# The gates' projections by Strassen's scheme on quarters, with two of four weight sums per block made by adding transfers

## The chip, the cores and the metric

One Trainium2 chip, one core of it. The metric is the time of one launch on the device in microseconds (us). The kernel before takes 1664.78 us, the median of 3 runs (1664.39 to 1664.81).

## What is computed

One layer of a decoder trunk over 512 tokens of width 2048, in fp32: a conditioned RMSNorm, one wide projection, two parallel mixers, gates, an output projection and a last RMSNorm.

```python
shift, scale, gate = split(silu(c) @ W_ada + b_ada)
h = rmsnorm(x, attn_norm_g) * (1 + scale) + shift
q_lat, kv_lat, k_rope, z_mla, u, v, z_sgu, g_mla, g_sgu = split(h @ w_in)
# widths:  768, 512, 64, then 2048 each for the last six
q  = rmsnorm(q_lat) @ w_uq            # 16 heads, 128 plain + 64 rotary
kv = rmsnorm(kv_lat) @ w_ukv          # 16 heads, 128 keys + 128 values
y_mla = causal_attention(q, rope(k), v) * silu(z_mla)
mixed = tril(w_spatial) @ rmsnorm(v) + b_spatial   # per chunk of 128 tokens, per group
y_sgu = u * mixed * silu(z_sgu)
merged = sigmoid(g_mla) * y_mla + sigmoid(g_sgu) * y_sgu
out = rmsnorm(x + gate * (merged @ w_out))
```

The change concerns the five "gates", of 2048 columns each: z_mla, g_mla, u, z_sgu and g_sgu. The code calls them types 0 to 4, and the kernel after calls them z, g, u, s, t. Each is h (512 x 2048) times a 2048 x 2048 part of w_in.

## The kernel before

**Number format.** Every fp32 matrix product is made of three matmuls of a reduced format: each operand x is a high part (`hi`, a cast on ACT) and a low part (`lo = x - hi`, a subtraction on DVE), and hi·hi + hi·lo + lo·hi is summed in PSUM. `mm3` (lines 134 to 136) issues the three.

**The stream of weights.** A `Stream` holds a list of weight granules in the order of their use; a granule is 128 x 1024 fp32 (512 KB) in the gates. SP issues its transfer into a raw tile (L76, `wraw`, 3 buffers), ACT casts it to `whi` (L97), DVE subtracts to `wlo` (L98), and PE uses the pair (2 buffers). `get(i, ahead=1)` splits one granule ahead of the one whose matmuls come next, and fills the free raw tiles.

**Stages**, by the time in the profiled execution:

- 0 to 74 us: the first columns of the latents, while DVE makes `shift` and `scale` from W_ada (`ada_dot`, 1 MB granules).
- 74 to 142: the rest of the latents; h is normalised and split on the way (`hh`, `hl`, 16 tiles of 128 x 512).
- 142 to 327: the v columns, in groups of 512, 512, 384, 384 and 320 columns.
- 327 to about 1203: the gates, 15 heads one after the other in this stage. A head has five types, a type two granules, and a granule 8 chunks of 128 x 128 weights, each times a 128 x 512 chunk of h: 16 x 3 matmuls of 512 columns a type, 240 a head. What is not of the gates lies beside: `shift_share` (L125: raw granules of the latents' weights times `shift`), the rotary tables (`rope_part`, small DVE operations, L122, L125, L129, L131), the SGU's mix (`sgu_prep`, `sgu_mix`, L675, L676), and from head 8 on the latents' norms.
- Then head 15's types t = 3, 4 (2 x 48 matmuls), the attention, head by head, and from about 1440 the output projection.

**Order.** The program's order is written by hand: each engine runs its own instructions in the order in which the code issues them. `pend` holds evacuations that run one granule later, `bg` the background steps, one for each granule. `evac` (L697 to 712) takes a type's 128 x 512 result out of PSUM: ACT makes the sigmoid, DVE multiplies it in. The gates' results are channel-major (channels on partitions) and stay in SBUF (`gt`, `vt`). All transfers go out from SP; POOL issues none.

## Time and profile before

| what | us |
|---|---|
| median of 3 runs | 1664.78 |
| the profiled execution | 1664.88 |
| its span | 1663.2 |
| PE busy in the span | 1651.6 |
| DVE busy | 947.5 |
| ACT busy | 583.3 |
| POOL busy | 2.2 |
| gates, 327.5 to 1200: the window, PE busy in it, DVE busy in it | 872.5, 872.5, 409.6 |

The profile is of one execution of the program. The busy time of an engine is the union of its instructions' times; PE's matmuls overlap in a pipeline, so a row's own duration (0.39 us for a matmul of 512 columns) is longer than the distance from one start to the next, and the distance is what a matmul costs. DVE's rows have such a tail too, of some 0.08 us. In the rows, `out<-in` gives the program's names of the tiles. A bracket at the end of a row tells how long the engine had been idle before and who ended that.

### The profile page before, as it was taken

How to read it: one execution, taken by the hardware profiler on the slowest of the kernel's cores; microseconds unless marked ns; L12 is line 12 of the kernel's file. 1: busy time of each engine (PE TensorE's matmuls, PEld its weight loads, DVE VectorE, ACT ScalarE, POOL GpSimd, SP SyncE). 2: the span in 40 equal slices, each digit the busy share in tenths (PEclk: the TensorE clock that was granted, in tenths of full speed). 3: DMA queues.
4: the chain of work that ended last, by engine and by line, in shares of the span. 5: the costliest groups of instructions: out<-in, count | busy, mean ns of one | idle time of the engine just before them, and what ended most of it. 6: DMA issues, size and time to landing. Idle time of an engine off the chain costs nothing.

```text
span 1663.2 us, 20082 instructions
## 1 busy us (share of the span) xinstructions
PE 1651.6 (99%) x8024; PEld 1406.1 (85%) x8024; DVE 947.5 (57%) x1456; ACT 583.3 (35%) x967; POOL 2.2 (0%) x11
## 2 busy tenths in 40 slices
PE   9999999999999999999999999999999999999998
PEld 7888889988888888888888888888898888888887
DVE  8988646365665644444443533323578778874453
ACT  4343333234223322221223322222455555542332
POOL 0000000000000000000000000000000000000000
PEclk9999999999999999999999999999999999999999
DMA  9878557344444333322222222232311221126332
GB/s 379 346 295 303 193 211 269 101 151 143 142 152 132 120 137 127 123 102 89 98 92 102 89 101 100 90 102 81 96 61 58 63 75 55 61 77 253 127 101 101
DMA packets 64508, 228.63 MB, mean 137 GB/s; under 512 B 7304, under 2 KB 9376, under 8 KB 57632
## 3 DMA queue, kind: packets, MB, share of 16 engines
q1 hardware_dynamic: 64416, 227.37, 38.7%
q8 instruction: 62, 1.02, 0.2%
q14 instruction: 30, 0.25, 0.0%
HBM read 223.14 MB, written 4.20 MB: 137 GB/s over the span
## 4 chain that ended last, share of the span: by engine, by line
PE 98%; DMA 1%; DVE 0%; ACT 0%; issue 0%; SPq 0%; DVEq 0%
PE ps L135 32%; PE ps L134 32%; PE ps L136 32%; PE ps L947 1%; PE ps L675 1%; PE ps L910 1%; PE ps L911 1%; DMA wraw<-in_w 1%; PE ps L676 0%; DMA wada<-in_c 0%; PE ps L606 0%; DVE wlo L98 0%; ACT whi L97 0%; PE ps L446 0%; DVE wada L122 0%
## 5 line engine op out<-in xcount | busy, mean ns | idle before, releaser
L98 DVE TENSOR_TENSOR wlo<-wraw,whi 128x1024 fp32r<-128x1024 f32 (+3 forms) x304 | 339.0, 1115 | 577.4 <-ACT whi L97 566.4
L134 PE MATMUL ps<-hh,whi 128*128 128x512 f32 x1640 | 641.6, 391 | 0.2 <-ACT hh L389 0.2
L135 PE MATMUL ps<-hl,whi 128*128 128x512 f32 x1640 | 638.5, 389 | 0.8 <-DVE hl L125 0.8
L136 PE MATMUL ps<-hh,wlo 128*128 128x512 f32 x1640 | 638.4, 389 | 0.0
L97 ACT CAST whi<-wraw 128x1024 fp32r<-128x1024 f32 (+3 forms) x304 | 293.7, 966 | 801.6 <-PE ps L135 561.0
L136 PEld LDWEIGHTS ps<-hh,wlo 128*128 128x128 f32 x1640 | 307.8, 188 | 64.5 <-DVE wlo L98 0.2
L135 PEld LDWEIGHTS ps<-hl,whi 128*128 128x128 f32 x1640 | 308.0, 188 | 64.0 <-DVE hl L125 1.1
L134 PEld LDWEIGHTS ps<-hh,whi 128*128 128x128 f32 x1640 | 307.9, 188 | 63.7 <-ACT hh L389 0.6
L134 PE MATMUL ps<-whi,hh 128*128 128x512 f32 (+3 forms) x448 | 148.9, 332 | 0.0
L135 PE MATMUL ps<-wlo,hh 128*128 128x512 f32 (+3 forms) x448 | 148.6, 332 | 0.1
L136 PE MATMUL ps<-whi,hl 128*128 128x512 f32 (+3 forms) x448 | 148.5, 332 | 0.0
L125 DVE SCALAR_TENSOR_TENSOR wada<-wada,cact 128x2048 f32<-128x2048 f32 x47 | 107.2, 2281 | 1.2 <-DMA wada<-in_wada 1.2
L135 PEld LDWEIGHTS ps<-wlo,hh 128*128 128x128 f32 x448 | 84.6, 189 | 5.4 <-DVE wlo L98 0.4
L136 PEld LDWEIGHTS ps<-whi,hl 128*128 128x128 f32 x448 | 84.6, 189 | 5.0
L134 PEld LDWEIGHTS ps<-whi,hh 128*128 128x128 f32 x448 | 84.6, 189 | 5.0
L134 PE MATMUL ps<-whi,b 128*128 128x512 f32 (+1 forms) x212 | 81.8, 386 | 0.0
L135 PE MATMUL ps<-wlo,b 128*128 128x512 f32 (+1 forms) x212 | 81.6, 385 | 0.0
L136 PE MATMUL ps<-whi,g 128*128 128x512 f32 (+1 forms) x212 | 81.6, 385 | 0.0
L134 PEld LDWEIGHTS ps<-whi,b 128*128 128x128 f32 x212 | 39.8, 188 | 7.9
L135 PEld LDWEIGHTS ps<-wlo,b 128*128 128x128 f32 x212 | 39.8, 188 | 7.9
L136 PEld LDWEIGHTS ps<-whi,g 128*128 128x128 f32 x212 | 39.8, 188 | 7.9
L139 ACT CAST lat<-ps 128x512 fp32r<-128x512 f32 (+1 forms) x64 | 35.4, 570 | 13.4 <-PE ps L136 13.3
(229 smaller groups left out, 1340.8 us busy)
## 6 DMA issues: line engine op xcount, KB each, us to landing
wraw<-in_wh SPq DMA_DIRECT2D x150, 512.0 KB, 3.3
wada<-in_wada SPq DMA_DIRECT2D x47, 1024.0 KB, 5.9
wraw<-in_w SPq DMA_DIRECT2D x32, 512.0 KB, 3.5
wraw<-in_wo SPq DMA_DIRECT2D x32, 512.0 KB, 3.3
wraw<-in_w SPq DMA_DIRECT2D x32, 320.0 KB, 2.9
wraw<-in_wv SPq DMA_DIRECT2D x16, 512.0 KB, 3.2
wraw<-in_wv SPq DMA_DIRECT2D x16, 384.0 KB, 3.3
wraw<-in_wq SPq DMA_DIRECT2D x16, 384.0 KB, 2.9
```

Source lines behind the costliest of these rows:

```text
L97: self.nc.scalar.copy(hi[:, :n], raw[:, :n])
L98: self.nc.vector.tensor_tensor(out=lo[:, :n], in0=raw[:, :n], in1=hi[:, :n].bitcast(F32), op=ALU.subtract)
L125: DVE.scalar_tensor_tensor(out=out, in0=in0, scalar=scalar, in1=in1, op0=op0, op1=op1, **kw)
L134: PE.matmul(ps, ah, bh, start=start, stop=False)
L135: PE.matmul(ps, ah, bl, start=False, stop=False)
L136: PE.matmul(ps, al, bh, start=False, stop=stop)
L139: ACT.copy(hi, src)
L675: PE.matmul(ps[:, n2], vh[:, n, :], whl[:, q], start=True, stop=False)
L910: PE.matmul(ps, q2[:, q], krh[:, :n], start=False, stop=False)
L911: PE.matmul(ps, q2[:, q], krl[:, :n], start=False, stop=True)
L947: PE.transpose(ps[:, o:o + P], pr_[i][:, j * P:(j + 1) * P], ident)
```

## The change

**Scheme.** For the gates, h and the weights are cut into quarters: two halves of the 2048 inputs (the first index of the weights' quarters), two halves of the tokens, and two halves of the columns (the second index). Strassen's scheme in Winograd's form multiplies two such 2 x 2 matrices with seven products of quarters in place of eight, from sums of quarters. 10 blocks (`BLOCKS`) cover the gates, each with two column halves of 512 (block 5: 320). A block has 28 items: seven products p1 to p7, each of four items i, and an item is 12 matmuls: 2 chunks x 2 groups of 128 tokens x 3 for hi and lo. The stationary operand is now a 128 x 128 piece of h (or of one of its sums), and the moving one a 128 x 512 piece of the weights. The results are token-major.

**Order of a block:** p1 x 4, p6 x 4, (2,0) (7,0) (2,1) (7,1) (2,2) (2,3) (7,2) (7,3), p3 x 4, p5 x 4, p4 x 4.

**The sums of weights.** For each i there is a tile `T` of 128 x 1024. Its first sum, w00 + w01, is made by transfers: SP loads w00, and a second transfer, issued by POOL, adds w01 to it in SBUF (`accum_op=ALU.add`). Both are issued when (1, i) is split; p6 uses the sum, four items later. Then DVE adds w11 to T (before p2), and w10 (after p5's split; p4 uses it). p3's operand, w01 + w11, is made in a raw tile, again by a load and an adding transfer. So a block has 8 adding transfers, or adding groups, and 8 additions on DVE. Block 5's granules, 640 columns, come in up to three pieces each. The gates' loads are now rows of 1 KB (`128x4x256`), not of 4 KB.

**The stream** has 4 raw tiles and 3 pairs of parts in the gates, and `get` is called with `ahead=2`. `form` makes the operand to be split, `after` is called behind the split, `keep` and `frees` hold a raw tile for a second use.

**What comes with it.** The sums of h (s1, s2, s4 in the v stage, s3 as background) are made on DVE. A finished product's banks are added up by `result` (DVE), and `gates` applies sigmoids and multiplies. z, u and s are token-major running products in DRAM scratch (`step_d`), written by one block and read by another. Types g and t are transposed on PE (124 transposes of 128 x 128, `turned`), copied by ACT and stored to `out_d`; the attention fetches them by head (`fetch`, 2 x 256 KB). v, the mix and the latents go through DRAM scratch too. The SGU's mix takes 48 matmuls of 512 columns in place of 64 pairs of 256 and 128. The shares of `shift` now lie in blocks 4 to 6, the rotary tables in blocks 5 and 6, the latents' norms in blocks 7 to 9. In all PE has 7672 rows in the program (8049 before), DVE 1729 (1403), ACT 1071 (838) and POOL 120 (17), of which 112 are adding transfers, 40.4 MB.

```diff
+BLOCKS = (
+    ((("z", 0, 512),), (("z", 512, 512),)),
+    ((("z", 1536, 384), ("g", 1024, 128)), (("z", 1024, 512),)),
+    ((("g", 0, 512),), (("g", 512, 512),)),
+    ((("u", 0, 512),), (("u", 512, 512),)),
+    ((("g", 1664, 256), ("u", 1664, 256)), (("g", 1152, 512),)),
+    ((("u", 1024, 320),), (("u", 1344, 320),)),
+    ((("s", 0, 512),), (("s", 512, 512),)),
+    ((("t", 0, 512),), (("t", 512, 512),)),
+    ((("s", 1024, 512),), (("s", 1536, 512),)),
+    ((("t", 1024, 512),), (("t", 1536, 512),)),
+)
...
+    def load(self, out, src, add):
+        if add:
+            self.nc.gpsimd.dma_start(out, src, accum_op=ALU.add)
+        else:
+            self.nc.sync.dma_start(out, src)
...
+            self.nc.scalar.copy(hi[:, :n], src)
+            self.nc.vector.tensor_tensor(out=lo[:, :n], in0=src, in1=hi[:, :n].bitcast(F32), op=ALU.subtract)
             self.hl[k] = (hi, lo)
-        for consume, raw in later:
+            if after is not None:
+                after(raws)
+            if not keep:
+                self.free(k)
+            if frees is not None:
+                self.free(frees)
...
...
             while j < len(self.src) and self.src[j][2] is not None:
                 j += 1
         self.split_to(j)
-        self.dma_to(self.n_split - 1 + self.raw_bufs)
+        self.dma_to(self.n_split + 6)
...
+        def first(i, b=b, w=w):
+            t = nt(c1[0].p, [P, GW], F32, f"T{i}")
+            T[i] = (b, t)
+            for at, src, add in w(0, 0, i) + w(0, 1, i, True):
+                ws.load(at(t), src, add)
...
+        def t_add(raws, i, n=n):
+            t = T[i][1][:, :n]
+            tt(t, t, raws[0][:, :n], ALU.add)
+            return t
...
+        def hold(raws, i, n=n, kept=kept):
+            kept[i] = raws[0][:, :n]
+            return t_add(raws, i, n)
+        seq = [(1, i) for i in range(4)] + [(6, i) for i in range(4)]
+        seq += [(2, 0), (7, 0), (2, 1), (7, 1), (2, 2), (2, 3), (7, 2), (7, 3)]
+        seq += [(p, i) for p in (3, 5, 4) for i in range(4)]
+        for p, i in seq:
+            if p == 1:
+                e = ws.add((w(0, 0, i),), n, after=lambda raws, f=first, i=i: f(i))
+            elif p == 2:
+                e = ws.add(w(1, 1, i), n, form=lambda raws, f=hold, i=i: f(raws, i), keep=True)
+                gc[b, i] = e
+            elif p == 7:
+                e = ws.add((), n, form=lambda raws, kept=kept, i=i: kept.pop(i), frees=gc[b, i])
+            elif p == 3:
+                e = ws.add((w(0, 1, i) + w(1, 1, i, True),), n)
+            elif p == 5:
+                e = ws.add(w(1, 0, i), n, after=lambda raws, f=t_add, i=i: f(raws, i))
+            else:
+                e = ws.add((), n, form=lambda raws, f=t_of, i=i: f(raws, i))
...
+    def turned(t, ty, n, c0, w):
+        ps = bank()[:, :w]
+        for q in range(w // P):
+            PE.transpose(ps[:, q * P:(q + 1) * P], t[:, q * P:(q + 1) * P], ident)
+        o = copy_slot()[:, :w]
+        ACT.copy(o, ps)
+        h0 = c0 % 1024 // P
+        DMA.dma_start(out_d[ty][c0 // 1024][h0:h0 + w // P, :, n * P:(n + 1) * P].rearrange("h p w -> p h w"),
+                      o.rearrange("p (h w) -> p h w", w=P))
...
+    def gates(all_):
+        tile_, n, pieces = open_.pop(0)
+        o, turns = 0, []
+        for ty, c0, w in pieces:
+            t, src = tile_[:, o:o + w], all_[:, o:o + w]
+            o += w
+            if ty != "u":
+                s_ = sig()[:, :w]
+                ACT.activation(s_, src, AF.Sigmoid)
+            if ty == "z":
+                tt(t, src, s_, ALU.mult)
+            elif ty == "u":
+                tt(t, src, t, ALU.mult)
+            else:
+                tt(t, t, s_, ALU.mult)
+                if ty == "s":
+                    tt(t, src, t, ALU.mult)
+            if ty in "gt":
+                turns.append((t, ty, n, c0, w))
+            else:
+                DMA.dma_start(piece_of(step_d, ty, n, c0, w), t)
+        if not turns:
+            later(2, open_next)
+            return
+        def turn():
+            for a in turns:
+                turned(*a)
+            later(1, open_next)
+        later(2, turn)
+    evs, bg = [], []
...
+    def make_s3(j):
+        a = sig()
+        tt(a, hh[j].bitcast(F32), hl[j].bitcast(F32), ALU.add)
+        tt(a[:, left], a[:, left], a[:, right], ALU.subtract)
+        hilo(hh[j][:, right], hl[j][:, right], a[:, left])
...
-        for t in range(5):
-            ps = bank()
-            for half in range(2):
-                wH, wL = get(gh[h, t, half], run=3 if h == 0 else 1)
-                if bg:
-                    bg.pop(0)()
-                for k in range(8):
-                    j = half * 8 + k
-                    sl = slice(k * P, (k + 1) * P)
-                    mm3(ps, wH[:, sl], wL[:, sl], hh[j], hl[j], j == 0, j == KC - 1)
-                if h < 8 and t == 0 and half == (h == 0):
-                    prep = sgu_prep(h)
-            pend.append(lambda h=h, t=t, ps=ps: evac(h, t, ps))
...
+    lefts = {1: quarter(0, 0), 2: sums_of("s2"), 3: quarter(0, 1), 4: quarter(1, 1), 5: quarter(1, 0),
+             6: sums_of("s1"), 7: sums_of("s4")}
...
+    for idx, (b, p, i, e) in enumerate(items):
...
+        wH, wL = ws.get(e, ahead=1 if ending else 2)
...
+        pair, lf = (y if p in (1, 2, 3, 4) else z), lefts[p]
+        for k in range(2):
+            for n in range(2):
+                fh, fl = lf(2 * i + k, n)
+                mh_, ml_ = moving(wH, b, k), moving(wL, b, k)
+                ps = pair[n][:, :w]
+                st = i == 0 and k == 0 and p in (1, 5, 6)
+                PE.matmul(ps, fh, mh_, start=st, stop=False, skip_group_check=True)
+                PE.matmul(ps, fh, ml_, start=False, stop=False, skip_group_check=True)
+                PE.matmul(ps, fl, mh_, start=False, stop=i == 3 and k == 1, skip_group_check=True)
+        if i == 3:
+            if p in (1, 2, 6):
+                base = {1: 0, 6: 2, 2: 4}[p]
+                store = [slot(f"lat{base + n}") for n in range(2)]
...
+            elif p == 7:
+                evs += [("u2", result("u2", z, u2, n, 1, w)) for n in range(2)]
+            elif p == 3:
+                evs += [("z6", result("z6", y, z6, n, 1, w)) for n in range(2)]
+            elif p == 5:
+                evs += [("p1", result("p1", z, p1, n, 0, w)) for n in range(2)]
+            elif p == 4:
+                evs += [("y", result("y", y, None, n, 0, w)) for n in range(2)]
...
+    def fetch(h):
+        vt[h] = nt(bp.p, [P, S], F32, f"b{h}")
+        DMA.dma_start(vt[h], out_d["t"][h // 8][h % 8])
+        gt[h] = nt((ga if h < 8 else g2p).p, [P, S], F32, f"g{h}")
+        DMA.dma_start(gt[h], out_d["g"][h // 8][h % 8])```

The rows below are the program's order on one engine, one instruction a row, with `out<-in` by the tiles' names and numbers and the output's shape. The first is DVE before, in head 8, where the latents' scaling (`lat`) runs in the background and `g` is the first gate.

```order
L98 TENSOR_TENSOR wlo_6294<-wraw_6155,whi_6293 128x1024
L122 TENSOR_TENSOR g_566_6213<-ps_6226,sig_6299 128x512
L122 TENSOR_TENSOR lat_24_106<-lat_24_106,rx_96 128x512
L98 TENSOR_TENSOR wlo_6328<-wraw_6231,whi_6327 128x1024
L122 TENSOR_TENSOR lat_25_107<-lat_25_107,rx_96 128x512
L98 TENSOR_TENSOR wlo_6360<-wraw_6265,whi_6359 128x1024
```

And DVE after, in block 3, items of p2, p7 and p3: `w0l`, `w1l`, `w2l` are the low parts (three pairs), `T` the sums, `wraw_168` to `wraw_173` raw granules; `wraw_172` and `wraw_173` are p3's sums, which POOL's transfers finish.

```order
L198 TENSOR_TENSOR T_535_5220<-T_535_5220,wraw_168_0_5310 128x1024
L167 TENSOR_TENSOR w0l_5488<-T_535_5220,w0h_5487 128x1024
L198 TENSOR_TENSOR T_539_5244<-T_539_5244,wraw_169_0_5341 128x1024
L167 TENSOR_TENSOR w2l_5505<-T_539_5244,w2h_5504 128x1024
L167 TENSOR_TENSOR w1l_5528<-wraw_168_0_5310,w1h_5527 128x1024
L167 TENSOR_TENSOR w0l_5547<-wraw_169_0_5341,w0h_5546 128x1024
L198 TENSOR_TENSOR rx_5484<-rx_5484,gsr_5386 128x512
L198 TENSOR_TENSOR sinT_5575<-rx_5484,cosT_5574 128x512
L167 TENSOR_TENSOR w2l_5579<-wraw_172_0_5409,w2h_5578 128x1024
L167 TENSOR_TENSOR w1l_5597<-wraw_173_0_5460,w1h_5596 128x1024
```

Where DVE made one low part of a granule and a result beside it, it now has the additions to `T` between the low parts, each ahead of the cast of what it made.

DVE after at the end of block 5, p5 and p4: the shares of `shift` (L201, on `rx` and `acc`) and the rotary tables (L205, L207, L198 on 128 x 128 tiles) stand between the low parts.

```order
L167 TENSOR_TENSOR w2l_7113<-wraw_256_0_7069,w2h_7112 128x640
L198 TENSOR_TENSOR T_635_6598<-T_635_6598,wraw_256_0_7069 128x640
L201 SCALAR_TENSOR_TENSOR rx_5868<-wraw_255_0_7041,shift_91,rx_5868 128x512
L201 SCALAR_TENSOR_TENSOR acc_17_96<-wraw_255_0_7041,shift_91,acc_17_96 128x128
L205 TENSOR_SCALAR lat_648_6761<-lat_648_6761 128x128
L207 TENSOR_SCALAR lat_649_6762<-lat_648_6761 128x128
L198 TENSOR_TENSOR lat_649_6762<-lat_648_6761,lat_649_6762 128x128
L205 TENSOR_SCALAR lat_648_6761<-lat_648_6761 128x128
L207 TENSOR_SCALAR lat_649_6762<-lat_648_6761 128x128
L198 TENSOR_TENSOR lat_648_6761<-lat_648_6761,lat_649_6762 128x128
L198 TENSOR_TENSOR lat_649_6762<-lat_649_6762,lat_648_6761 128x128
L167 TENSOR_TENSOR w1l_7145<-T_624_6497,w1h_7144 128x640
```

Before, such a step stood in front of one granule's low part at a time, over the first seven heads.

POOL after, the first six of its eight in block 3: the adding transfers for the four `T` and for p3's raw tiles.

```order
L138 DMA T_527_5161<-in_wh 128x4x256
L138 DMA T_532_5194<-in_wh 128x4x256
L138 DMA T_535_5220<-in_wh 128x4x256
L138 DMA T_539_5244<-in_wh 128x4x256
L138 DMA wraw_172_0_5409<-in_wh 128x4x256
L138 DMA wraw_173_0_5460<-in_wh 128x4x256
```

Before, POOL issued no transfer; each of these takes the place of an addition that DVE would have had.

785 lines of the change are left out of this document (539 added, 246 removed).

## The prediction

> **What bounds the kernel now.** I read the page's busy times and chain first, then the windows by stage, which also bring DVE, ACT and the DMA engines.
>
> ```profile
> span 1663.2 us, 20082 instructions
> PE 1651.6 (99%) x8024; PEld 1406.1 (85%) x8024; DVE 947.5 (57%) x1456; ACT 583.3 (35%) x967; POOL 2.2 (0%) x11
> PE 98%; DMA 1%; DVE 0%; ACT 0%; issue 0%; SPq 0%; DVEq 0%
> ...
> 0.00:74.00 74.00, 70.30 (x368) 58.85 (x369) 64.08 (x89) 32.46 (x45) 2.19 (x11) 1.00 0.97 385
> 74.00:142.00 68.00, 68.00 (x300) 55.94 (x299) 61.02 (x71) 26.59 (x39) 0.00 (x0) 1.00 0.78 293
> 142.00:327.50 185.50, 185.50 (x956) 168.31 (x955) 105.73 (x114) 65.00 (x146) 0.00 (x0) 1.00 0.57 206
> 327.50:1200.00 872.50, 872.50 (x3943) 726.28 (x3942) 409.63 (x595) 257.43 (x332) 0.00 (x0) 1.00 0.33 113
> ```
>
> The chain is 98% PE. In the gates (the last row; its numbers behind the window are busy time and count of PE, PEld, DVE, ACT and POOL, then granted clock, DMA share, GB/s) PE is busy for all of the 872.5 us at full clock, DVE for 47%, the DMA engines for 33%. So a matmul taken out of the gates is time taken out, as long as something else can deliver what the remaining ones need. The change takes matmuls and spends DVE time, transfers and a queue that has done nothing so far. The question is what is left of the gain.
>
> **The matmuls.** A matmul's price is its distance to the next one on PE's timeline.
>
> ```profile
> 362.83 0.39 PE L136 MATMUL ps<-hh,wlo 128*128 128x512 f32 x1
> ...
> 367.82 0.39 PE L134 MATMUL ps<-hh,whi 128*128 128x512 f32 x1
> ...
> 309.83 0.31 PE L134 MATMUL ps<-whi,hh 128*128 128x320 f32 x1
> ...
> 312.18 0.31 PE L135 MATMUL ps<-wlo,hh 128*128 128x320 f32 x1
> ```
>
> The first pair of rows is 22 matmuls apart: 4.99 / 22 = 0.2268 us for 512 columns. The second pair is 16 apart: 2.35 / 16 = 0.1469 for 320; those are the v columns, which already have h as the stationary operand, as the gates will have. Out go 15 heads x 240 + 96 = 3696 matmuls of 512, 838.3 us. In come 10 blocks x 28 items x 12 = 3360: 3024 of 512 (685.8) and, in block 5, 336 of 320 (49.4). That is **-103.1**.
>
> ```profile
> 787.16 1.58 PE L606 MATMUL ps<-ident,acc 128*128 128x128 f32 x13
> 788.57 0.60 PE L757 MATMUL ps<-ident,krn 128*128 128x128 f32 x4
> ...
> 358.63 0.34 PE L675 MATMUL ps<-whl,vh 128*128 128x256 f32 x1
> ...
> 359.79 0.33 PE L675 MATMUL ps<-whl,vh 128*128 128x256 f32 x1
> ```
>
> 13 transposes start 1.41 us before the next ones: 0.108 each. 130 are new (124 of the gates' results, six of small tables and keys): **+14.1**. The SGU's pairs of 256 and 128 columns are 1.16 / 5 = 0.232 apart; 64 pairs go (14.8), 48 matmuls of 512 come (10.9): **-3.9**. PE's sum is -92.9, so with PE never waiting the profiled execution of 1664.88 (0.1 above the median, so no correction) comes to **1572**.
>
> **DVE's load per block.** A block of 512 columns now lasts 336 x 0.2268 = 76.2 us on PE, 79 to 82 with its transposes and its part of the mix; block 5 lasts 49.4. I add up DVE's instructions block by block in the program's order, at these prices:
>
> ```profile
> 801.00 1.22 DVE L98 TENSOR_TENSOR wlo<-wraw,whi 128x1024 fp32r<-128x1024 f32 x1 [3.61 <-ACT whi L97]
> 802.14 0.68 DVE L122 TENSOR_TENSOR g<-ps,sig 128x512 f32<-128x512 f32 x1
> 802.74 0.68 DVE L122 TENSOR_TENSOR lat<-lat,rx 128x512 f32<-128x512 f32 x1
> ...
> 111.79 0.82 DVE L98 TENSOR_TENSOR wlo<-wraw,whi 128x640 fp32r<-128x640 f32 x1
> 112.52 0.94 DVE L456 RECIPROCAL rx<-rx 128x128 f32<-128x128 f32 x1
> ...
> 367.98 1.28 DVE L125 SCALAR_TENSOR_TENSOR acc<-wraw,shift,acc 128x1024 f32<-128x1024 f32 x1
> 369.18 0.22 DVE L129 TENSOR_SCALAR rd<-rb 128x128 f32<-128x128 f32 x1
> 369.43 0.23 DVE L131 TENSOR_SCALAR re<-rd 128x128 f32<-128x128 f32 x1
> 369.70 0.29 DVE L122 TENSOR_TENSOR rd<-rd,re 128x128 f32<-128x128 f32 x1
> 370.02 0.29 DVE L122 TENSOR_TENSOR rs<-rs,rd 128x128 f32<-128x128 f32 x1
> ```
>
> From start to start that is 1.14 us for 1024 elements, 0.73 for 640, 0.60 for 512, 1.20 for a share, and 0.28 for a small operation ((370.02 - 369.18) / 3). An ordinary block has 28 low parts (31.9), 8 additions (9.1) and its results and gates: in all 56 to 64 us of work, and 81 in block 6, 69.5 in block 8, where shares, or sums and latents, come on top. Most blocks fit under PE's 79. Blocks 5 and 6 do not: 28 x 1.14 + 28 x 0.73 = 52.4 of low parts, 8 x 1.14 + 8 x 0.73 = 15.0 of additions, some 20 of shares, 136 small operations of the rotary tables x 0.27 to 0.28 = 37, some 18 of results: 142 us against PE's 125.6.
>
> On top come waits that an addition brings: DVE adds to T, ACT must cast the sum, and only then can DVE make the low part. The order has nothing for DVE between the two at most of these places.
>
> ```profile
> 799.91 1.05 ACT L97 CAST whi<-wraw 128x1024 fp32r<-128x1024 f32 x1 [4.38 <-PE ps L135]
> 800.86 0.59 ACT L697 ACTIVATE sig<-ps 128x512 f32<-128x512 f32 x1
> ```
>
> Eight casts of about 1.05 and some eight sigmoids of 0.6 make about 13 in the two blocks. So 155 against 125.6, 29 us too much, of which two items of lead (2.7 us each) take off a little: +27. Block 8, 69.5 + 12 of such waits against PE's 76.2 (it has no transposes), gives +4 after its lead. The **DVE term is +31**. Its lower bound takes no waits, 142 - 125.6 = 16; its upper one no lead in blocks 5 and 6 and the full 12 us of such waits in one more block, 29 + 4 + 12 = 45. I take 31, since the order leaves DVE little to do in these gaps.
>
> The sums s1, s2 and s4 of h are new in the v stage: for each of 8 chunks one operation of 512 and nine of 256 (between the 0.28 and the 0.60 above, say 0.4), 8 x 4.2 = 34 us. The stage (its row is above) has DVE idle for 185.5 - 105.7 = 79.8: 0, and without this cover 34.
>
> **The adding transfers.** No row shows one. The nearest are the loads:
>
> ```profile
> wraw<-in_wh SPq DMA_DIRECT2D x150, 512.0 KB, 3.3
> wada<-in_wada SPq DMA_DIRECT2D x47, 1024.0 KB, 5.9
> ...
> wada<-in_wada SPq DMA_DIRECT2D x15, 1024.0 KB, 11.0
> wraw<-in_w SPq DMA_DIRECT2D x15, 512.0 KB, 9.4
> ...
> wada<-in_wada SPq DMA_DIRECT2D x13, 1024.0 KB, 5.5
> wraw<-in_w SPq DMA_DIRECT2D x16, 320.0 KB, 3.5
> ...
> 335.68 0.33 SPq L76 DMA_DIRECT2D wraw<-in_wh  x1
> ```
>
> The last column is the median time from issue to landing, the first two rows over the whole run, the next two in the first 74 us, where the DMA share is 0.97, the last two from 74 to 142, where it is 0.78. A sum of 512 KB is a load and, behind it, an adding transfer. The lower bound takes the second at the price of a plain one: 0.33 + 3.3 + 0.33 + 3.3 = 7.3. With the second at the price of 1024 KB it is 9.9; with both under full engines 0.66 + 9.4 + 11.0 = 21.1. What is there: the load goes out when (1, i) is split, p6's item is split four items later, 4 x 2.72 = 10.9, and its matmuls are two items behind that, 16.3, less 1.05 and 1.23 for cast and low part: 14.0 before PE waits. A block's bytes, some 17 MB by SP and 4.2 by POOL (8 x 512 KB), counted twice for the adding ones, are 25.4 MB. Full engines would move that in 74 us by the gates' row (113 / 0.33 = 342 GB/s) and in 64 by the first stage's (385 / 0.97 = 397); over a block of 80 us that is a share of 0.80 to 0.92. At 0.78 the 1024 KB row still lands in 5.5, so between 7.3 and 21.1 I take 9.9: hidden, **0**. What could spend the difference is SP's queue: between two loads stand stores of gates (L782, L794) that wait for a result from DVE or ACT, and behind a waiting store the next T's load, and so its adding transfer on POOL, wait as well. 4.1 us of such waiting are free.
>
> [...]
>
> Two small terms: block 5's sums come in three pieces each, three loads and three adding transfers one behind the other (+4, bounds 0 and 8 x 0.66 = 5), and at the end of the gates the latents and the first heads' gates are fetched back from DRAM before the attention (+3, one transfer's landing of 3.3). The other loads and stores fit under PE's 76 to 82 us a block as said, barely, so 0; without that cover they cost what the third rival says.
>
> Sum: 1664.9 - 92.9 + 31 + 4 + 3 = 1610, called **1612** with the first block's start, where nothing is loaded ahead for p1's partners (one landing, 3.3, half hidden).
>
> **Rivals.**
>
> *Adding transfers come late (slower).* POOL's queue takes them one by one, 8 a block; the page shows 11 instructions of it and no issue, so its pace is unknown. If a T lands 7.2 us too late (the 21.1 against 14.0), PE waits at the first T and at p3's first sum, both in all ten blocks: 2 x 10 x 7.2 = 144, which gives 1612 + 144 = 1756. The gain of 53 is gone from 53 / 20 = 2.7 us late, that is at 16.7 from first issue to landing. Against it: the rows at 0.78, and POOL has 76 us for eight. For it: rows of 1 KB, an unknown queue, and SP's stores ahead of the loads. Chance 0.30.
>
> [...]
>
> *Everything hides.* The waits for ACT fall into time DVE would idle, and shares and tables spread over what the neighbours have free; then only 6 us of the small terms are left: 1578. For it: before, DVE idles 53% of the gates. Against it: 142 over 125.6 with no wait at all. Chance 0.13.
>
> *The DMA engines become the bound.* [...] Block 4 moves 20.5 MB by SP and 4.2 x 2 by POOL, 28.9 MB / 342 = 84 us against 79; blocks 8 and 9 the same. That alone is 3 x 5 = 15 us; with rows of 1 KB a tenth dearer than those of 4 KB it is 92 against 78, 3 x 14 = 42 beside the forecast, about 1650. For it: the first stage shows what full engines do to a landing (9.4 against 3.3). Against it: at the first stage's 397 GB/s block 4 too takes only 73. Chance 0.12.
>
> **How the numbers follow.** Forecast 0.42, late transfers 0.30, all hidden 0.13, full engines 0.12, rest 0.03. The likeliest one's own range is 1590 to 1640 (DVE 16 to 45, transfers late by an us in some blocks). The range reaches down to the all-hidden case and up into the late transfers as far as 4.4 us a time (1612 + 20 x 4.4): **1575 to 1700**; what lies above is about half of that rival, 0.15, and the rest. About 0.2%, 3.3 us, is what a measurement of this kernel can tell from no change. Forecast and all hidden are faster (0.55); of full engines, whose landings stretch too, three quarters (0.09) and of the late transfers 0.04; another 0.02 of these are level, and what is left, 0.24 + 0.03 and the rest's 0.03, is slower: faster 0.68, same 0.02, slower 0.30.
>
> **What would show it.** PE's matmuls of 512 columns still at 0.227 from start to start, 3360 of them in the gates, from about 327 to about 1130. In blocks 5 and 6 (about 720 to 870) DVE busy over 90% and PE waiting on low parts; elsewhere PE without gaps. POOL's adding transfers landing within 7 us of their issue, and no idle time of ACT or DVE that ends with a T's transfer. Wrong if PE waits at p6 or p3 in every block, if the gates' DMA share is above 0.9, or if matmuls with a strided moving operand are dearer than 0.227.

## The result, and the profile after

The changed kernel takes 1905.86 us, the median of 4 runs (1901.3 to 1910.3), beside 1664.63 for the kernel before: 1.1449 times as long, 95% interval 1.1412 to 1.1486. The forecast was 1612. The profiled execution took 1910.3.

The page of the changed kernel, the lines that answer to those shown of before, with its rows of the granted clock and of the DMA share (40 slices, in tenths):

```profile
span 1908.6 us, 21480 instructions
PE 1681.0 (88%) x7738; PEld 1378.8 (72%) x7738; DVE 1231.5 (65%) x1786; ACT 772.8 (40%) x1244; POOL 140.9 (7%) x123
...
PEclk9999999899999999888898899999899999999999
DMA  9886785778767888778683887977774222225332
...
PE 49%; DMA 24%; DVE 14%; ACT 7%; issue 5%; SPq 2%; POOL 0%; ACTq 0%; DVEq 0%; POOLq 0%
...
wraw<-in_wh SPq DMA_DIRECT2D x112, 512.0 KB, 5.7
...
T<-in_wh SPq DMA_DIRECT2D x28, 512.0 KB, 7.0
T<-in_wh POOLq DMA_DIRECT2D x28, 512.0 KB, 10.8
wraw<-in_wh POOLq DMA_DIRECT2D x28, 512.0 KB, 7.2
```

The chain that was 98% PE is now half PE and a quarter DMA. The windows by stage say where (columns as in the prediction):

```profile
142.00:341.50 199.50, 197.12 (x1017) 178.70 (x1016) 147.25 (x208) 73.83 (x131) 0.00 (x0) 0.99 0.69 234
341.50:1436.00 1094.50, 881.28 (x3555) 681.41 (x3554) 647.76 (x824) 430.82 (x612) 138.69 (x112) 0.91 0.77 196
1436.00:1908.00 472.00, 463.93 (x2505) 403.46 (x2503) 311.33 (x596) 209.07 (x420) 0.00 (x0) 0.99 0.34 113
```

The gates run from 341.5 to 1436, 1094.5 us. Before, their first matmul came at 336.7, and 3696 x 0.2268 and the mix bring their end to some 1190, 853 us. So the gates took about 240 us more, the stage ahead of them 5 more, and what follows the same: nearly all of the loss is in the gates. PE is busy for 881 of them and idle for 213, and its granted clock is 0.91.

I cut PE's timeline into the 280 items and took from each item's length (from its first matmul to the next item's first) its 12 matmuls (12 x 0.2268, in block 5 12 x 0.1469). What remains is loss, 359 us in the whole, of which some 25 are transposes and the mix, which stand in these items. By product, in us over all ten blocks, for the changed kernel and for the runs told below:

| run | us | p1 | p6 | p2 | p7 | p3 | p5 | p4 | sum |
|---|---|---|---|---|---|---|---|---|---|
| the change | 1905.9 | 33 | 106 | 31 | 43 | 81 | 49 | 16 | 359 |
| e1_no_second | 1727.8 | 14 | 25 | 31 | 20 | 18 | 56 | 13 | 178 |
| e5_no_sums | 1670.8 | 16 | 17 | 9 | 19 | 13 | 30 | 15 | 120 |
| e4_pool_copies | 1820.2 | 20 | 66 | 33 | 41 | 41 | 52 | 16 | 269 |
| e9_half_add | 1812.6 | 18 | 63 | 31 | 39 | 42 | 54 | 16 | 263 |
| e7_4kb_rows | 1851.4 | 22 | 88 | 30 | 41 | 54 | 52 | 14 | 301 |
| e3_T_earlier | 1875.5 | 77 | 25 | 28 | 43 | 74 | 54 | 24 | 325 |
| e8_spread | 1884.8 | 42 | 74 | 25 | 42 | 76 | 52 | 23 | 333 |
| e73_4kb_earlier | 1831.3 | 64 | 15 | 30 | 41 | 62 | 48 | 21 | 281 |
| e2_dve_sums | 1900.3 | 81 | 17 | 31 | 30 | 122 | 50 | 20 | 351 |
| e7d_4kb_dve | 1860.3 | 67 | 15 | 28 | 28 | 104 | 53 | 16 | 310 |
| r3_no_tables | 1869.2 | 30 | 110 | 20 | 33 | 75 | 38 | 12 | 319 |

p6 is the first to use T, and p3 uses the other sum that transfers make: together 187. So counted, a wait ahead of a product's first item stands in the product before it: 18 of p1's 33 us lie ahead of p6's first item, and 19 of p7's 43 ahead of p3's first. Booked to the item that waits, p6 and p3 have 219 in the changed kernel and 40 in e1.

POOL's timeline in block 1 of the changed kernel shows how one such wait comes about (a row's bracket: idle time ahead of it, and who ended it):

```profile
451.26 1.26 POOL L138 DMA_DIRECT2D T<-in_wh  x1 [42.07 <-DVE w1l L167]
452.74 1.28 POOL L138 DMA_DIRECT2D T<-in_wh  x1 [0.21 <-issue]
462.29 1.26 POOL L138 DMA_DIRECT2D T<-in_wh  x1 [8.28 <-DMA T<-in_wh]
466.34 1.28 POOL L138 DMA_DIRECT2D T<-in_wh  x1 [2.79 <-DMA T<-in_wh]
```

And ACT's, at the same place:

```profile
464.85 1.05 ACT L166 CAST w0h<-T 128x1024 fp32r<-128x1024 f32 x1 [3.55 <-DMA T<-in_wh]
...
472.13 1.04 ACT L166 CAST w2h<-T 128x1024 fp32r<-128x1024 f32 x1 [4.68 <-DMA T<-in_wh]
```

POOL issues the third sum's transfer only when SP's load of it has landed (462.29, after 8.28 us of waiting), and ACT can cast it at 472.13, 9.8 later. PE has nothing until then:

```profile
469.62 0.39 PE L1239 MATMUL ps<-w0h,s1l 128*128 128x512 f32 x1
473.23 0.80 PE L1237 MATMUL ps<-w2h,s1h 128*128 128x512 f32 x1 [3.22 <-ACT w2h L166]
474.49 0.80 PE L1238 MATMUL ps<-w2l,s1h 128*128 128x512 f32 x1 [0.46 <-DVE w2l L167]
475.08 0.63 PE L1239 MATMUL ps<-w2h,s1l 128*128 128x512 f32 x1
475.51 0.63 PE L1237 MATMUL ps<-w2h,s1h 128*128 128x512 f32 x1
```

It waits for 3.22 us, and then its matmuls are 0.43 apart in place of 0.227, to the end of the item.

The windows of that same block 1, p1 to p4 in the order of the program, explain the late landings (the last three numbers are granted clock, DMA share, GB/s; the first row begins two items early, when T's loads go out):

```profile
445.70:462.70 17.00, 17.00 (x77) 14.08 (x76) 10.59 (x12) 8.46 (x13) 2.95 (x3) 1.00 0.96 232
462.70:483.80 21.10, 15.79 (x52) 10.91 (x51) 7.19 (x7) 8.60 (x14) 2.13 (x2) 0.84 0.82 198
483.80:510.90 27.10, 25.00 (x104) 18.77 (x103) 18.36 (x20) 15.67 (x26) 5.10 (x4) 1.00 0.69 164
510.90:527.00 16.10, 13.12 (x49) 9.97 (x48) 7.24 (x9) 4.32 (x6) 0.00 (x0) 0.89 0.99 236
527.00:547.90 20.90, 15.59 (x53) 11.43 (x51) 14.44 (x16) 8.99 (x15) 0.00 (x0) 0.84 0.58 170
547.90:559.10 11.20, 11.20 (x52) 9.16 (x51) 7.03 (x9) 6.12 (x11) 0.92 (x1) 1.00 0.43 126
```

The DMA engines are full in p1 (0.96) and p3 (0.99), and 0.43 to 0.69 in p2, p7, p5 and p4; the block's mean is 0.75. Over the ten blocks p1's stretch has 0.97 and p3's 0.90 in the mean. In p1 the engines move only 232 GB/s, where full engines in the first stage before moved 385: most of the difference goes into adding (3.51 us of all the engines for 512 KB, against 1.72 for a load, as worked out next), some into the rows of 1 KB (1.72 for a load against 1.56 with rows of 4 KB, e7 below). The queues of the changed kernel in the gates (MB, share of the time of 16 engines), SP's and then POOL's:

```profile
q1 hardware_dynamic: 179341, 173.27, 51.8%
q0 software_dynamic: 46848, 40.38, 24.7%
```

Over 1095 us that is 305 GB/s for a full share of SP's queue, 1.72 us for 512 KB, and 149 GB/s for POOL's, 3.51 us. Each i of p1 asks for a granule, a load of T and an adding transfer, 1.72 + 1.72 + 3.51 = 6.95 us of all the engines, and PE takes 2.72 for an item.

The two queues together have 76.5% of 1095 us, 838 us of engine time (the time of their packets), or 84 a block, where PE's matmuls, transposes and mix need 76. So the mean share of 0.77 leaves room only because the gates had become longer: in the forecast's gates of some 800 us the same transfers would make a share of 1.04 (an estimate).

At p3 the lead is short as well. p3's sums are made in raw tiles, and SP's load goes out only when a tile is free; over the whole run SP's loads waited 328.8 and 296.4 us for two of DVE's low parts (w1l and w0l). From the load's issue to the landing of the adding transfer these sums took 12.6 us in the median, but the third and fourth of a block are begun late. In block 3, where p3 began at 723.0, the third item was due at 728.4 and its cast and low part 2.28 earlier, 11.7 behind this load:

```profile
714.41 0.37 SPq L140 DMA_DIRECT2D wraw<-in_wh  x1
...
721.09 1.26 POOL L138 DMA_DIRECT2D wraw<-in_wh  x1 [10.09 <-DVE w2l L167]
...
730.75 1.04 ACT L166 CAST w0h<-wraw 128x1024 fp32r<-128x1024 f32 x1 [9.38 <-DMA wraw<-in_wh]
```

The sum took 16.3 us, and PE waited 3.27.

### The profile page after: what moved, and what is told of

Read it like the earlier page. It is cut to its first block, busy times and chain, and to the rows that moved or that the text cites. A ratio compares the mean times of both kernels' runs of the same rounds, so it can differ in the third digit from the quotient of the medians.

```text
span 1908.6 us, 21480 instructions
## 1 busy us (share of the span) xinstructions
PE 1681.0 (88%) x7738; PEld 1378.8 (72%) x7738; DVE 1231.5 (65%) x1786; ACT 772.8 (40%) x1244; POOL 140.9 (7%) x123
## 2 busy tenths in 40 slices
DMA  9886785778767888778683887977774222225332
## 3 DMA queue, kind: packets, MB, share of 16 engines
q0 software_dynamic: 46848, 40.38, 14.2%
## 4 chain that ended last, share of the span: by engine, by line
PE 49%; DMA 24%; DVE 14%; ACT 7%; issue 5%; SPq 2%; POOL 0%; ACTq 0%; DVEq 0%; POOLq 0%
PE ps L211 13%; PE ps L212 13%; PE ps L210 13%; DMA wraw<-in_wh 8%; DMA T<-in_wh 6%; PE ps L1238 3%; PE ps L1239 3%; PE ps L1237 3%; DVE T L198 3%; DMA rx<-lat_d 2%; DVE lat L198 2%; DVE w0l L167 2%; DMA latn_d<-rx 2%; DVE w2l L167 2%; ACT w0h L166 2%
## 5 line engine op out<-in xcount | busy, mean ns | idle before, releaser
L167 DVE TENSOR_TENSOR w1l<-wraw,w1h 128x1024 fp32r<-128x1024 f32 (+3 forms) x127 | 135.5, 1067 | 118.1 <-ACT w1h L166 117.3
L167 DVE TENSOR_TENSOR w0l<-wraw,w0h 128x1024 fp32r<-128x1024 f32 (+2 forms) x127 | 142.2, 1119 | 94.1 <-ACT w0h L166 93.4
L166 ACT CAST w0h<-wraw 128x1024 fp32r<-128x1024 f32 (+2 forms) x127 | 123.0, 968 | 152.5 <-PE ps L212 47.5
L166 ACT CAST w1h<-wraw 128x1024 fp32r<-128x1024 f32 (+3 forms) x127 | 117.2, 923 | 155.3 <-PE ps L212 43.4
L138 POOL DMA_DIRECT2D T<-in_wh x56 | 69.5, 1420 | 820.2 <-DMA T<-in_wh 654.9
L201 DVE SCALAR_TENSOR_TENSOR wada<-wada,cact 128x2048 f32<-128x2048 f32 x47 | 107.2, 2281 | 0.0
L1237 PE MATMUL ps<-w1h,hh 128*128 128x512 f32 (+1 forms) x212 | 87.1, 411 | 19.8 <-ACT w1h L166 19.8
L1237 PE MATMUL ps<-w2h,hh 128*128 128x512 f32 (+1 forms) x212 | 87.1, 411 | 16.5 <-ACT w2h L166 16.5
L138 POOL DMA_DIRECT2D wraw<-in_wh x56 | 69.1, 1532 | 422.4 <-DMA wraw<-in_wh 261.7
L1238 PE MATMUL ps<-w1l,hh 128*128 128x512 f32 (+1 forms) x212 | 86.3, 407 | 12.3 <-DVE w1l L167 12.3
L1237 PE MATMUL ps<-w0h,hh 128*128 128x512 f32 (+1 forms) x216 | 88.0, 407 | 9.8 <-ACT w0h L166 9.7
L210 PE MATMUL ps<-w0h,hh 128*128 128x256 f32 (+3 forms) x288 | 93.6, 325 | 1.0 <-ACT w0h L166 1.0
L198 DVE TENSOR_TENSOR T<-T,wraw 128x1024 f32<-128x1024 f32 (+1 forms) x80 | 94.3, 1179 | 0.0
L211 PE MATMUL ps<-w0l,hh 128*128 128x256 f32 (+3 forms) x288 | 93.3, 324 | 1.0 <-DVE w0l L167 1.0
L212 PE MATMUL ps<-w0h,hl 128*128 128x256 f32 (+3 forms) x288 | 93.0, 323 | 0.0
L1238 PE MATMUL ps<-w0l,hh 128*128 128x512 f32 (+1 forms) x216 | 87.4, 405 | 6.0 <-DVE w0l L167 6.0
L167 DVE TENSOR_TENSOR w2l<-wraw,w2h 128x1024 fp32r<-128x1024 f32 (+1 forms) x52 | 61.1, 1175 | 48.6 <-ACT w2h L166 48.0
L198 DVE TENSOR_TENSOR lat<-lat,lat 128x512 f32<-128x512 f32 (+4 forms) x122 | 66.6, 549 | 39.9 <-ACT lat L806 35.4
L167 DVE TENSOR_TENSOR w1l<-T,w1h 128x1024 fp32r<-128x1024 f32 (+1 forms) x39 | 46.1, 1183 | 71.2 <-ACT w1h L166 71.2
L1238 PE MATMUL ps<-w2l,hh 128*128 128x512 f32 (+1 forms) x212 | 86.2, 406 | 6.7 <-DVE w2l L167 6.7
L167 DVE TENSOR_TENSOR w2l<-T,w2h 128x1024 fp32r<-128x1024 f32 (+1 forms) x41 | 48.9, 1193 | 59.9 <-ACT w2h L166 59.9
## 6 DMA issues: line engine op xcount, KB each, us to landing
wraw<-in_wh SPq DMA_DIRECT2D x112, 512.0 KB, 5.7
wraw<-in_w SPq DMA_DIRECT2D x32, 512.0 KB, 6.0
wraw<-in_wo SPq DMA_DIRECT2D x32, 512.0 KB, 3.5
T<-in_wh SPq DMA_DIRECT2D x28, 512.0 KB, 7.0
T<-in_wh POOLq DMA_DIRECT2D x28, 512.0 KB, 10.8
wraw<-in_wh POOLq DMA_DIRECT2D x28, 512.0 KB, 7.2
```

The source lines that it names most:

```text
L138: self.nc.gpsimd.dma_start(out, src, accum_op=ALU.add)
L166: self.nc.scalar.copy(hi[:, :n], src)
L167: self.nc.vector.tensor_tensor(out=lo[:, :n], in0=src, in1=hi[:, :n].bitcast(F32), op=ALU.subtract)
L198: DVE.tensor_tensor(out=out, in0=in0, in1=in1, op=op)
L201: DVE.scalar_tensor_tensor(out=out, in0=in0, scalar=scalar, in1=in1, op0=op0, op1=op1, **kw)
L210: PE.matmul(ps, ah, bh, start=start, stop=False)
```

## The experiments

Theory L: the sums land late. Theory D: DVE's additions and round trips with ACT cost it. Theory E: the DMA engines' time does. Each run is one profiled launch; the kernel before took 1664.4 to 1665.4 beside them. The changed kernel itself ranged over 9 us, so smaller differences say nothing.

**e1_no_second.** The second operand is left out of both sums:

```diff
-            for at, src, add in w(0, 0, i) + w(0, 1, i, True):
+            for at, src, add in w(0, 0, i):
...
-                e = ws.add((w(0, 1, i) + w(1, 1, i, True),), n)
+                e = ws.add((w(0, 1, i),), n)
```

> The second operand of both sums that transfers make is left out (T starts as w00, p3 uses w01 alone): no adding transfer is issued, PE, ACT and DVE do the same work. Theory L (the sums land late: a load, then POOL's issue, then the adding transfer): PE's loss at p6 and p3, 187 us of the 334 that the gates lose beyond matmuls, transposes and mix, goes; 1906 - 187 + some 15 that stay = about 1735. Theory D (the additions on DVE and the round trips between DVE and ACT): nothing of that is touched, 1880 or more. Theory E (the DMA engines are too full for loads to land in time): 4.2 of some 21 MB a block go, and these cost twice, so p6 and p3 gain about a third, 1840.

Measured 1727.8: 178 us go, 144 of them at p6 and p3 (179 booked to the item that waits). L. Why the sums are late this run doesn't tell, since the engine time of adding goes with them. And 1728 is still 63 above the kernel before, so it isn't all.

**e5_no_sums.** Beside that, `t_add` returns T without adding.

```diff
             t = T[i][1][:, :n]
-            tt(t, t, raws[0][:, :n], ALU.add)
             return t
```

> As the run without the second operand, and DVE's two additions to T are left out too: no sum of weights is made at all, DVE has 8 operations of 1024 a block less, and ACT's casts no longer wait for DVE. Loads and PE's work are the same. Theory D (the additions' round trips between DVE and ACT make what is left of the loss, most of it at p5 and p2): 1728 - 70 = about 1660. Theory E (loads that land late make it): 1715 or more.

Measured 1670.8: another 57, most of it from p5 and p2 (26 and 22), as D has it for this part. With no sum of weights at all the seven products only draw level with the kernel before (1664.6 beside it).

**e2_dve_sums.** The two sums made by DVE from two raw tiles each.

```diff
-            for at, src, add in w(0, 0, i) + w(0, 1, i, True):
-                ws.load(at(t), src, add)
+            tt(t[:, :n], raws[0][:, :n], raws[1][:, :n], ALU.add)
...
+        def both(raws, n=n):
+            t = raws[0][:, :n]
+            tt(t, t, raws[1][:, :n], ALU.add)
+            return t
...
-                e = ws.add((w(0, 1, i) + w(1, 1, i, True),), n)
+                e = ws.add((w(0, 1, i), w(1, 1, i)), n, form=both)
```

> All four sums of weights on DVE: w00 and w01, and w01 and w11, are loaded into two raw tiles each and added by DVE; no adding transfer. The full computation. L: the loss at p6 and p3 goes (-170), eight more DVE additions a block (9 us, ten blocks) come where DVE has about 40% idle, of which the waits for ACT may cost 30: about 1770. D: DVE's additions were the cost, and there are twice as many: slower than 1906, 1940 or more. Loads two raw tiles ahead in place of four may cost either theory some tens of us more.

Measured 1900.3, the same as with the transfers. The loss at p6 goes (106 to 17) and comes back where two raw tiles are wanted per item: p1 33 to 81, p3 81 to 122. The expectation's last sentence had allowed some tens of us for it; it cost as much as the late sums had. My reading, not tested: a raw tile is held for its landing (5.0 here), cast and low part, some 7.3 us, and four tiles at two an item give an item every 3.7 us, not 2.72. A fifth raw tile was not tried.

**e3_T_earlier.** T's load and adding transfer are issued behind (4, i) of the block before.

```diff
-                e = ws.add((w(0, 0, i),), n, after=lambda raws, f=first, i=i: f(i))
+                e = ws.add((w(0, 0, i),), n, after=(lambda raws, f=first, i=i: f(i)) if b == 0 else None)
...
+                           after=(lambda raws, b=b, i=i: firsts[b + 1](i)) if p == 4 and b + 1 < len(BLOCKS) else None)
```

> T's first load and its adding transfer are issued behind the split of (4, i) of the block before, four items (10.9 us) earlier; otherwise the same, the full computation. L: p6's loss (106 us) shrinks to about 15, p3's stays: about 1815. E: the landings get longer by what they are issued earlier, about 1900. D: no change, 1900.

Measured 1875.5: p6 falls to 25 as L says, but p1 rises from 33 to 77. T's transfers now stand ahead of p1's granules; what was put first made the next late. That is E's picture, though E had expected no gain at all.

**e4_pool_copies.** POOL's transfers copy in place of adding.

```diff
-            self.nc.gpsimd.dma_start(out, src, accum_op=ALU.add)
+            self.nc.gpsimd.dma_start(out, src)
```

> POOL's transfers copy in place of adding (the sum of the two quarters is left out, T and p3's operand are the second quarter alone); the same queue, chain and count, but the destination is not read. L with the chain as its cause (two landings behind one another and POOL's issue): 1880 to 1906. [...]

Measured 1820.2, 86 less, and below the 1880 of the chain alone: the addition's own price is about half of the 178, the second transfer behind the first the other half. The queues in its gates (341 to 1350), and the landings:

```profile
q1 hardware_dynamic: 179782, 174.42, 55.5%
q0 software_dynamic: 11648, 40.38, 12.1%
...
T<-in_wh POOLq DMA_DIRECT2D x28, 512.0 KB, 7.5
wraw<-in_wh POOLq DMA_DIRECT2D x28, 512.0 KB, 5.2
```

The same 40.38 MB now take 12.1% of 1009 us: 331 GB/s, 1.58 us for 512 KB against 3.51 when they are added. They also go in a quarter of the packets (11648 against 46848), so this run alone doesn't part the addition from the smaller packets; in e7 the adding transfers go in 11520 packets and still take 2.87 us.

**e7_4kb_rows.** The gates' weights lie in memory as the granules want them, so each transfer has rows of 4 KB.

```diff
...
+    def quarter_of(b, kh, ch, i, add=False):
+        n = 2 * width(b)
+        src = wh15[kh, ch, i] if b == 5 else wh[b - (b > 5), kh, ch, i]
+        return [(lambda x, n=n: x[:, :n], src, add)]
...
```

> The full change, with the gates' weights laid out in memory as its granules want them: each load and each adding transfer of 512 KB is one piece with rows of 4 KB a partition, in place of 1 KB rows in up to three pieces. Theory E (the DMA engines' time for small rows makes loads and sums late): landings of plain loads fall from 5.7 us towards 4 and the loss at p6 and p3 halves: about 1800. Theory C (the chain itself, two landings and POOL's issue of 1.4 us, whatever the rows): 1880 to 1905.

Measured 1851.4: 54 less, of which p3 27 and p6 18. C falls, and E has half of what it claimed: the plain loads of 512 KB landed in 5.2, not in 4. **e73_4kb_earlier** has both edits:

> Rows of 4 KB, and T's load and adding transfer four items earlier, the full computation. E: with both, p6 and p1 lose little and p3 half of its 81: about 1760. C: the earlier issue alone helps, about 1870.

Measured 1831.3, the best of the full computation by the changed scheme, between E's 1760 and C's 1870: p6 falls to 15, but p1 again pays (64), and p3 keeps 62 where E had half of 81. **e7d_4kb_dve**, rows of 4 KB with e2's sums on DVE:

> All four sums on DVE and rows of 4 KB. E: each pair of raw tiles is there sooner, 1900 - 80 = about 1820. C says nothing of it; if the two raw tiles an item (of four) and DVE's additions set the loss, 1880 or more.

Measured 1860.3, between the two; the raw tiles' part stays.

**r1_probe.** What an adding transfer costs by itself: extra pairs in the kernel before, where nothing waits.

```diff
+                self.nc.sync.dma_start(v, first)
+                if add:
+                    self.nc.gpsimd.dma_start(v, second, accum_op=ALU.add)
+                else:
+                    self.nc.gpsimd.dma_start(v, second)
```

> The kernel before with 40 extra pairs of transfers in heads 7 to 14, where nothing else needs them: SP loads 512 KB into a raw tile, POOL puts a second 512 KB on it. Four kinds in turn: pa adds with rows of 1 KB, pb copies with rows of 1 KB, pc adds with rows of 4 KB, pd copies with rows of 4 KB. Nothing of the result changes; PE should stay busy (1665 to 1675). The DMA share is about 0.35 there. If an adding transfer is slow by itself, pa lands 7 us or more after its issue; if it was slow for the traffic in the changed kernel's gates, pa lands within 5.5, some 2 us behind pb (3.5).

Measured 1664.9, and these landings from 890 to 1200 us, where the DMA share was about 0.6:

```profile
pc<-in_wh POOLq DMA_DIRECT2D x7, 512.0 KB, 6.3
...
pd<-in_wh POOLq DMA_DIRECT2D x6, 512.0 KB, 3.6
...
pa<-in_wh SPq DMA_DIRECT2D x6, 512.0 KB, 4.3
pa<-in_wh POOLq DMA_DIRECT2D x6, 512.0 KB, 6.2
...
pb<-in_wh POOLq DMA_DIRECT2D x6, 512.0 KB, 4.4
```

An adding transfer lands in 6.2, between the two expectations; with its load the sum takes 4.3 + 6.2 = 10.5. In the changed gates it is 7.0 + 10.8 = 17.8.

**r5_pairs, e9_half_add, e8_spread** ask why. Theory P: adding transfers under way together slow each other. Theory Tr: the gates' other traffic slows them. r5 puts transfers of 256 KB alone and in pairs into the kernel before:

> The kernel before with extra transfers in heads 7 to 14 again, rows of 2 KB, nothing waits for them: a load of 512 KB, and then on it one adding transfer of 256 KB (pa), two of 256 KB one right behind the other (pb), one of 512 KB (pc), or four of 128 KB (pd). PE should stay busy (1665 to 1668). P: pa alone lands in about 4.5 us and pb's second in 6 or more; Tr: pb's both land like pa, since the engines are only 0.6 busy.

```profile
pb<-in_wh POOLq DMA_DIRECT2D x20, 256.0 KB, 5.8
...
pc<-in_wh POOLq DMA_DIRECT2D x10, 512.0 KB, 5.3
pa<-in_wh POOLq DMA_DIRECT2D x10, 256.0 KB, 3.7
```

Measured 1665.2. One lands in 3.7, two in 5.8 (median of both), somewhat longer than one of twice the size (5.3): P, and 256 KB more cost 1.6 us. The four of 128 KB land in 4.2 (median of all). That the two of a pair share the DMA engines' time would explain it as well. e9 adds only the first half of each transfer's rows:

```diff
+            k = out.shape[1] // 2
+            self.nc.gpsimd.dma_start(out[:, :k], src[:, :k], accum_op=ALU.add)
```

> The adding transfers move only the first half of their rows (half of the second operand is left out of both sums): as many transfers, at the same places, 2 MB a block less of 21. P: each takes half as long, overlapped ones land in about 6 us, and the loss at p6 and p3 (187) falls by more than half: about 1800. Tr: a tenth of the traffic goes, about 1880. If the chain of issues alone made it late, 1890 or more.

Measured 1812.6, 93 less with as many transfers, p6 and p3 from 187 to 105. It is the adding bytes, not the number of issues. e8 spreads the four T over twice the time:

> The full change, with the four T's loads and adding transfers spread: T0 and T1 are issued behind (4,0) and (4,2) of the block before, T2 and T3 behind (1,0) and (1,2), two items (5.4 us) apart in place of one. Theory P (POOL's adding transfers slow each other when two are under way: 6.0 us to landing alone, 10.3 overlapped, in the changed kernel's own trace): T's landings fall from 10.8 to 7 or 8 us, the loss at p1 and p6 from 139 to about 70, the time to about 1835. Theory Tr (the other traffic of the gates makes every adding transfer slow): landings stay above 10, and the time is that of the run with all four earlier, about 1875.

Measured 1884.8: P's 1835 falls. T's adding transfers still land in 10.2 there, and p1 and p6 keep 116 of 139. But the edit hardly got them apart: a sum takes 17 us and they are begun 5.4 apart, and only 3 of T's 28 adding transfers of 512 KB had no other beside them. Those 3 landed in 9.2, with the engines 0.96 busy; in the changed kernel 10 of p3's had none beside them and landed in 6.0, with the engines 0.73 busy. So landings go with how full the engines are, and whether adding transfers slow each other beyond that isn't shown.

Less engine time does help. The engine time of both queues in the gates, and the time of the run, are 838 and 1906 us for the change, 736 and 1851 for e7, 692 and 1813 for e9, 682 and 1820 for e4, 559 and 1728 for e1. e2, with 627 and 1900, stands apart: it makes no adding transfers, and by the reading above its raw tiles set the pace.

**r3_no_tables.** The sums of 30 of the 32 shares and the middle of the rotary tables are left out:

```diff
-                else:
-                    stt(acc[0], raw, shift[:, k:k + 1], acc[0], ALU.mult, ALU.add)
...
-                    else:
-                        stt(a, raw[:, sl], shift[:, j:j + 1], a, ALU.mult, ALU.add)
...
-        rope.extend([s0, s1, s2, lambda: frac("c", c1_, True), lambda: frac("c", c2_),
-                     lambda: frac("b", d1 / 65536.0), lambda: frac("b", d2 / 65536.0), s7, s8, s9, s10])
+        rope.extend([s0, s9, s10])
```

> The change without the sums of the 32 shares (only the first of each set is made) and with the rotary tables cut to their first and last operations: DVE has some 57 us less in blocks 4 to 6, the loads are unchanged; shares and tables come out wrong. If DVE's load makes blocks 4, 5 and 6 lose more than the others (41, 48 and 52 us against 31 on average), they fall to about 31 and the time by 45, to about 1860. If the landings make it, less than 15 us are gained.

Measured 1869.2, 37 less. The loss of blocks 4, 5 and 6 falls from 41, 48 and 52 to 35, 35 and 33, the level of the others. That part of DVE's cost is real.

**r4_filled.** 24 transposes of the identity ahead of four items a block.

```diff
+        if p in (6, 3) and i in (1, 2):
+            fill = bank()
+            for _ in range(24):
+                PE.transpose(fill[:, :P], ident, ident)
```

> The change with 24 transposes of the identity (2.6 us, never read) put ahead of the items (6,1), (6,2), (3,1) and (3,2) of each block, where PE waits for 3 to 6 us. If PE's slow matmuls behind a wait (0.43 us in place of 0.227) come from its idling, fewer of them follow, and the time falls by 10 to 30 us; if they don't, the fillers cost where the wait was shorter, and it rises by up to 40.

Measured 1938.7, 33 more. Matmuls at 0.28 to 0.46 from start to start fall from 328 to 241, so the slow clock does follow the idling. p6 kept its loss (105) with 52 us of fillers in it, so they ran in time that was lost anyway; p3 rose by 25. The fewer slow matmuls brought nothing here, where the next sum was late too.

## Why the prediction was wrong

**The matmuls** were right: 0.227 from start to start with a strided moving operand, 3360 of them, and the stages around the gates cost what they did, but for 5 us ahead of the gates, where the sums of h were taken to be hidden.

**The step that failed** is "so between 7.3 and 21.1 I take 9.9: hidden, **0**". The price was near for an adding transfer beside lighter traffic (10.5 in r1, share 0.61). Its error was the sum ahead of it: 25.4 MB, 64 to 74 us of engine time, a share of 0.80 to 0.92 "over a block of 80 us". The runs showed 84 us a block, as 512 KB took 3.51 for adding and 1.72 for a load. And the transfers aren't spread over a block: T's loads and sums fall into p1, p3's into p3, and in those stretches the engines were 0.97 and 0.90 busy. There T's sum took 17.8 against the 14.0 at hand, and four of them queued (16.8, 18.7, 20.9 and 23.8 in block 3). The 14.0 was worked out for T alone; p3's third sum had 11.7 in that block and took 16.3. So items waited anew: 187 us at p6 and p3, 178 by leaving the adding out.

Rival 1 had the place and the mechanism; its 1756 was 7.2 us late at two places a block, and the runs showed 10.6 at p6 and 8.1 at p3 (106 and 81 over ten blocks) on top of the rest. The break-even of 2.7 us was passed at both. Rival 3, full engines, had the engine time right: 92 us for block 4 and for 8 and 9, with small rows a tenth dearer; the trace has 89, 92 and 87, and 1.72 us against e7's 1.56. Its 28.9 MB and the 25.4 MB above count an adding transfer's bytes twice. No run shows them moved twice; in engine time the runs showed 2.0 times a load of the same rows (3.51 us against 1.72 for 512 KB) and 2.2 times a copy (1.58, e4). The rival made 42 us of its engine time, by whole blocks, without the bursts. Of the prediction's signs of being wrong, PE waited at p6 in every block; the gates' share stayed at 0.77, since the gates had become longer.

**The DVE term**, +31, was right in place, short in size. DVE was busy for 58.8 + 84.3 = 143 us in blocks 5 and 6, where 142 was worked out, and the shares and tables cost 37 (r3). What was missing: the additions cost in ordinary blocks too, 57 by e5 against e1, most of it at p5 and p2. At p2 the cast waits for the addition, a round trip from DVE to ACT and back. At p5 no cast does: the additions stand between the low parts, where DVE is 0.77 busy in e1 and 0.65 in e5 (from two items ahead of p5 to its last). e5 takes both away, so how much the round trips cost isn't shown.

**Never counted** were the seams. e5 has no sums and still loses 95 us in the gates beside transposes and mix; the prediction allowed 7 beside DVE's term. Its trace puts the first of it on low parts and on gates' results that aren't there when their transposes are due:

```profile
PE ps L1236 <- DVE w0l L167: 16.1, 13, 7.8
PE ps L1236 <- DVE w1l L167: 11.9, 12, 2.7
PE ps L788 <- DVE lat L198: 9.4, 4, 4.3
PE ps L1236 <- DVE w2l L167: 7.3, 9, 1.5
```

(waits of PE in e5: total, times, longest; L1235 and L1236 are its item's matmuls, L788 the transposes). The idle time of PE in its gates is 60; the rest is matmuls that come further apart than 0.227, which this table can't part.

And the clock: the sum took 0.227 for every matmul, and 328 of the changed kernel's came at 0.28 to 0.46, some 55 us more in all. Two windows around the wait of 3.22 us shown above (granted clock, DMA share and GB/s are last; a packet is counted whole where it starts, so a short window's share can pass 1):

```profile
469.19:472.60 3.41, 0.82 (x4) 0.36 (x2) 0.00 (x0) 0.47 (x1) 0.00 (x0) 1.00 1.20 228
472.60:479.40 6.80, 5.71 (x12) 3.77 (x12) 3.10 (x3) 3.08 (x7) 0.00 (x0) 0.50 0.61 137
```

The granted clock is 0.50 from 472.6 to 479.4, and the item's matmuls come 0.427 apart. In the 3.41 us before, PE was busy for 0.82 (24%). In the gates the granted clock falls to 0.50 36 times, for 3.4 or 6.8 us at a time, and PE was busy for 0 to 52% of the 3.41 us ahead of each. r4 shows that this did not set the time at p6: slow matmuls fell to 241 from 328, and p6's loss stayed 105.

**POOL's pace**, which rival 1 called unknown: an issue of 512 KB on POOL took 1.28 us in the median in the changed kernel, at most 1.53, and 1.29 to 1.32 for the same form in r1. Only pieces issued one behind another in block 5 took longer, up to 3.67 us. POOL was busy for 138.69 of the gates' 1094.50 us.

No version that was run beats the kernel before.

## What to carry to other kernels

Add up the engine time of all transfers at measured prices and hold it against the stage as it will be, not as it was: here 84 us a block against PE's 76. A mean share also says little about a schedule that asks for its transfers in bursts, so do the same for the stretch between issue and use: here 0.77 over the gates, but 0.97 in p1 and 0.90 in p3. An adding transfer here took 2.2 times the engine time of a plain copy (3.51 us against 1.58 for 512 KB), or 1.8 times that of a plain load where both have rows of 4 KB (2.87 against 1.56), and a sum is a chain of two landings (7.0 + 10.8 us for T). Work out the lead of each sum by itself, with the buffer that its load has to wait for. And when a PE-bound stage is cut by an eighth, each helper's slack shrinks with it: leave the new work out first (here, no sums at all) to see whether the shorter stage pays even when that work is free.

## What the runs showed of the hardware

Adding 512 KB to SBUF by POOL's queue took 3.51 us of all 16 DMA engines with rows of 1 KB, copying it 1.58. In e7, rows of 4 KB:

```profile
q1 hardware_dynamic: 95562, 173.24, 49.7%
q0 software_dynamic: 11520, 40.38, 21.3%
```

Over 1037 us that is 183 GB/s and 2.87 us for adding, 336 GB/s and 1.56 us for plain loads (1.72 with small rows). POOL's own time for one issue was 1.29 us for adding with rows of 1 KB, 0.79 for copying them, 0.89 for adding with rows of 4 KB and 0.57 for copying those:

```profile
1048.09 1.29 POOL L81 DMA_DIRECT2D pa<-in_wh  x1 [8.39 <-DVE wlo L110]
1060.22 0.79 POOL L83 DMA_DIRECT2D pb<-in_wh  x1 [10.84 <-DMA pb<-in_wh]
1069.63 0.89 POOL L81 DMA_DIRECT2D pc<-in_wh  x1 [8.62 <-DVE wlo L110]
1083.04 0.57 POOL L83 DMA_DIRECT2D pd<-in_wh  x1 [12.51 <-DMA pd<-in_wh]
```

(POOL's timeline in r1: start, duration.) And PE's granted clock was 0.50 from 472.6 to 479.4, behind 3.41 us in which PE was busy for 0.82, and its matmuls of 512 columns came 0.427 apart there in place of 0.227; over the gates the slow matmuls cost some 55 us beside 213 of idle time.
